# L2 pooling in windows of four: one instruction per load instead of two halves

## The chip, the cores and the metric

The kernel runs on one core of a Trainium2 chip. The metric is the device time of one execution in microseconds (us), the median of the runs shown. Four parts of the core matter here. ACT (ScalarE) and DVE (VectorE) are the engines that compute. SP (SyncE) computes nothing here and only issues transfers. The 16 DMA engines move data between HBM and SBUF.

## The reference

The input x has shape 32 x 256 x 4096 in float32, p is 2 and the window is 4. Each output element is the root of the mean of four squares:

```python
for i in range(out_length):                     # out_length = 4096 // 4
    window = np.abs(x[:, :, 4 * i:4 * i + 4]) ** 2.0
    result[:, :, i] = np.mean(window, axis=-1) ** 0.5
```

134.2 MB are read and 33.6 MB are written. Windows never cross a row, so the whole input can be treated as one flat run of windows.

## The kernel before, in words

The flat input is cut into 20 loads. Loads 0 to 18 bring 13184 elements (`W`) to each of 128 partitions, 6592 KB in all; load 19 brings the remaining 11648 per partition (`LAST`). Three slots in SBUF (`x_tiles`, shown as `xt`) take the loads in turn: load i goes to slot i mod 3. Load 0 is cut in two parts, the first of 1024 elements per partition on ACT's DMA queue. All other loads are issued on SP's queue.

The order on each engine is written out by hand, and each engine works through its own list in that order. For loads 0 to 17 the loop does the following, in two halves of 6592 elements per partition each:

- `square` (line 101, ACT) squares a half in place.
- `pairs` (line 107, DVE) adds elements 0 and 2, and 1 and 3, of each window, and writes the result in place to the front of the half.
- `fours` (line 111, DVE) adds the two sums of each window and writes 1648 elements to PSUM, to one of two tiles (`s_tiles`, shown as `st`), one for each half.
- `root` (line 114, ACT) scales by 1/4, takes the root and writes to the output tile `o_tile` (shown as `ot`). `roots(i)` runs both halves' roots.

`roots(i - 1)` stands on ACT between the two squares of load i. For i = 5, 9, 13 and 17 (`waits`) it stands behind both squares, and the pair sums of both halves come ahead of the sums of four, since at these places the root may have to wait.

`fours` of load i may overwrite the PSUM sums only when the roots of load i - 1 have read them. When `fours` of load i is done, its slot is free, and SP issues load i + 3 (line 87).

The output tile holds the results of four loads. The blocks of loads that are stored together are [0-3], [4-7], [8-11], [12, 13], [16, 17, 14, 15], [18] and [19]. Stores 0 to 3 are issued on ACT's queue (line 98), directly behind `roots` of loads 3, 7, 11 and 13. The first root of the next block writes where the store still reads, so it waits for the store to land.

The tail differs. Load 18 is squared in two parts, the first 5560 elements by a multiplication on DVE (line 151), the others on ACT. Load 19 goes through in three pieces of 6912, 3152 and 1584 elements. Stores 4, 5 and 6 (6592, 1648 and 1456 KB) are issued on SP's queue, behind `roots(17)`, behind the root of load 18, and behind the last root. The results of loads 18 and 19 lie in the slot of load 17.

Of the kernel before, what the change touches and what calls it, by code (L numbers as in the profile page):

```python
# [1 line left out]

# [4 lines left out]


@with_exitstack
def kernel(  # L10
    ctx: ExitStack,
    tc: tile.TileContext,
    x: bass.AP,
    p: float,
    kernel_size: int,
    out: bass.AP,
):

    nc = tc.nc

    assert float(p) == 2.0, "kernel specialized for p == 2"
    k = int(kernel_size)  # L30
    assert k == 4, "kernel specialized for kernel_size == 4"

    P = nc.NUM_PARTITIONS
    fp32 = mybir.dt.float32
    Act = mybir.ActivationFunctionType
    add = mybir.AluOpType.add
    xf = x.rearrange("b c l -> (b c l)")
    of = out.rearrange("b c l -> (b c l)")
    total = xf.shape[0] // P

    W = 13184
    H, R = W // 2, W // k
    X_SLOTS = 3
    EARLY = 1024
    LAST = total - 19 * W
    widths = [W] * 19 + [LAST]
    n = len(widths)
    assert 0 < LAST <= W and LAST % 16 == 0


    blocks = [[0, 1, 2, 3], [4, 5, 6, 7], [8, 9, 10, 11], [12, 13], [16, 17, 14, 15], [18], [19]]
    block_of = {i: b for b, loads in enumerate(blocks) for i in loads}
    block_width = [sum(widths[i] for i in loads) for loads in blocks]

    x_pool = ctx.enter_context(tc.tile_pool(name="x_pool", bufs=1))
    o_pool = ctx.enter_context(tc.tile_pool(name="o_pool", bufs=1))
    s_pool = ctx.enter_context(tc.tile_pool(name="s_pool", bufs=1, space=bass.MemoryType.PSUM))
    x_tiles = [x_pool.tile([P, W], fp32, name=f"xt{j}") for j in range(X_SLOTS)]
    o_tile = o_pool.tile([P, 4 * R], fp32, name="ot")
    first = o_pool.tile([P, 1], fp32, name="first")  # L60
    s_tiles = [s_pool.tile([P, 2048], fp32, name=f"st{j}") for j in range(2)]
    ctx.enter_context(tc.manual_schedule())

    def rows(flat, b, div):
        at = sum(block_width[:b]) * P // div
        return flat[at:at + block_width[b] * P // div].rearrange("(p w) -> p w", p=P)


    place = {}
    for b, loads in enumerate(blocks):  # L70
        for q, i in enumerate(loads):
            if i < 18:
                place[i] = o_tile[:, q * R:(q + 1) * R]
    free = x_tiles[17 % X_SLOTS]
    place[18] = free[:, 0:R]
    place[19] = free[:, R:R + LAST // k]

    xs = {}

    def load(i):  # L80
        b = block_of[i]
        at = sum(widths[j] for j in blocks[b][:blocks[b].index(i)])
        xs[i] = x_tiles[i % X_SLOTS][:, 0:widths[i]]
        cuts = [0, widths[i]] if i else [0, EARLY, W]
        queues = [nc.sync] if i else [nc.scalar, nc.sync]
        for queue, c, e in zip(queues, cuts, cuts[1:]):
            queue.dma_start(out=xs[i][:, c:e], in_=rows(xf, b, 1)[:, at + c:at + e])  # L87

    def store(b, queue):
        if b <= 2:  # L90
            held = o_tile[:, :]
        elif b == 3:
            held = o_tile[:, 0:2 * R]
        elif b == 4:
            held = o_tile[:, :]
        else:
            held = place[blocks[b][0]]
        queue.dma_start(out=rows(of, b, k), in_=held)

    def square(v):  # L100
        nc.scalar.activation(out=v, in_=v, func=Act.Square)  # L101

    def pairs(v):

        q = v.rearrange("p (n j) -> p n j", j=k)
        h = v[:, 0:v.shape[1] // 2].rearrange("p (n j) -> p n j", j=2)
        nc.vector.tensor_tensor(out=h, in0=q[:, :, 0:2], in1=q[:, :, 2:4], op=add)  # L107

    def fours(o, v):
        h = v[:, 0:v.shape[1] // 2].rearrange("p (n j) -> p n j", j=2)  # L110
        nc.vector.tensor_tensor(out=o, in0=h[:, :, 0], in1=h[:, :, 1], op=add)  # L111

    def root(o, s):
        nc.scalar.activation(out=o, in_=s, func=Act.Sqrt, scale=1.0 / k)  # L114

    def roots(i):
        for c in range(2):
            root(place[i][:, c * R // 2:(c + 1) * R // 2], s_tiles[c][:, 0:R // 2])
        if i in (3, 7, 11, 13):
            store(block_of[i], nc.scalar)  # L120

    for i in range(X_SLOTS):
        load(i)

    nc.vector.memset(first[:, :], 1.0)  # L125
    root(first[:, :], first[:, :])
    for i in range(18):
        halves = [xs[i][:, c * H:(c + 1) * H] for c in range(2)]
        waits = i > 1 and (i - 1) % 4 == 0
        square(halves[0])  # L130
        if i and not waits:
            roots(i - 1)
        square(halves[1])
        if waits:
            roots(i - 1)
            for v in halves:
                pairs(v)
            for c, v in enumerate(halves):
                fours(s_tiles[c][:, 0:R // 2], v)
        else:  # L140
            for c, v in enumerate(halves):
                pairs(v)
                fours(s_tiles[c][:, 0:R // 2], v)
        if i + X_SLOTS < n:
            load(i + X_SLOTS)
    roots(17)


    c = 5560
    v = xs[18][:, 0:c]  # L150
    nc.vector.tensor_tensor(out=v, in0=v, in1=v, op=mybir.AluOpType.mult)  # L151
    square(xs[18][:, c:W])
    store(4, nc.sync)
    for a, b in ((0, c), (c, W)):
        pairs(xs[18][:, a:b])
        fours(place[18][:, a // k:b // k], xs[18][:, a:b])
    ends = [0, 6912, 10064, LAST]
    for a, b in zip(ends, ends[1:]):
        v = xs[19][:, a:b]
        o = place[19][:, a // k:b // k]  # L160
        square(v)
        if a == 0:
            root(place[18], place[18])
            store(5, nc.sync)
        pairs(v)
        fours(o, v)
        if a:
            root(*last)
        last = (o, o)
    root(*last)  # L170
    store(6, nc.sync)


# [1 line left out]
_INS = ['x', 'p', 'kernel_size']  # L175
_OUTS = [((32, 256, 1024), 'float32')]

_NUMBERS = {'p': 2.0, 'kernel_size': 4}


# [26 lines left out]
```

## Time and profile before

| | |
|---|---|
| Time, median of 3 runs | 394.63 us (394.58 to 394.68) |
| Span of the profiled execution, first to last instruction | 392.7 us; its time outside the span is not in the profile |
| ACT busy | 279.3 us, 82 instructions |
| DVE busy | 223.4 us, 84 instructions |
| HBM read, written | 134.22 MB, 33.55 MB; 427 GB/s over the span |
| SP's DMA queue, ACT's DMA queue | 143.62 MB, 24.15 MB |

A profile line of a group of instructions gives the line of the kernel, the engine, the operation, what is written and read with their shapes (partitions x elements), the number of instructions, the busy time in us and the mean time of one in ns, and then the idle time of the engine just before them and what ended it. A line of DMA issues gives the tensors, the queue, the number, the size and the median time from issue to landing. In the timeline and in the chain of waits, the first two numbers are the start and the length in us, both from the start of the span.

### The profile page before, as it was taken

To read this page: it belongs to the slowest core of one execution; us is meant where nothing else is said; L and a number is where in the kernel's file an instruction comes from. 1 tells how busy PE (TensorE), PEld (TensorE's weight loads), DVE (VectorE), ACT (ScalarE), POOL (GpSimd) and SP (SyncE) were. 2 spreads that over 40 slices of the span, in tenths; PEclk is the share of its full clock that TensorE was granted. 3 is DMA by queue.
4 is the path that set the end of the run, shared out by engine and by line. 5 is a ranking of instruction groups with operands and counts; after the bars stand their busy time and mean duration, and the time that the engine had idled before them with its cause. 6 is when DMAs were issued, how large, how long until landed. Compare 5 with 4: busy or idle time off the path is not lost.

```text
span 392.7 us, 311 instructions
## 1 busy us (share of the span) xinstructions
DVE 223.4 (57%) x84; ACT 279.3 (71%) x82; POOL 0.2 (0%) x4
## 2 busy tenths in 40 slices
DVE  0046586766460567664606667645166654669992
ACT  1095988987650999876419898773297929897792
POOL 0000000000000000000000000000000000000000
DMA  8999999999999999999999999999999999999997
GB/s 337 436 430 430 430 440 440 435 457 376 430 430 430 446 430 440 430 440 440 446 430 436 435 435 431 435 430 430 430 430 419 457 414 430 435 429 451 415 428 320
DMA packets 4034, 167.79 MB, mean 427 GB/s; under 512 B 448, under 2 KB 448, under 8 KB 576
## 3 DMA queue, kind: packets, MB, share of 16 engines
q1 hardware_dynamic: 3312, 143.62, 84.9%
q10 hardware_dynamic: 720, 24.15, 14.2%
q14 instruction: 2, 0.02, 0.0%
HBM read 134.22 MB, written 33.55 MB: 427 GB/s over the span
## 4 chain that ended last, share of the span: by engine, by line
DMA 73%; ACT 17%; DVE 6%; issue 2%; SPq 0%; ACTq 0%; DVEq 0%
DMA xt<-in_x_dram 46%; DMA out_dram<-ot 27%; ACT xt L101 12%; ACT ot L114 5%; DVE xt L107 3%; DVE st L111 2%; DVE xt L111 1%; ACT xt L114 1%; SPq L87 0%; ACTq L101 0%; DVEq L107 0%; ACTq L114 0%
## 5 line engine op out<-in xcount | busy, mean ns | idle before, releaser
L101 ACT ACTIVATE xt<-xt 128x6592 f32<-128x6592 f32 (+4 forms) x40 | 221.4, 5547 | 61.2 <-DMA xt<-in_x_dram 59.6
L107 DVE TENSOR_TENSOR xt<-xt 128x3296 f32<-128x3296 f32 (+5 forms) x41 | 143.1, 3489 | 125.0 <-ACT xt L101 124.7
L111 DVE TENSOR_TENSOR st<-xt 128x1648 f32<-128x1648 f32 x36 | 67.4, 1882 | 36.0 <-ACT ot L114 34.1
L114 ACT ACTIVATE ot<-st 128x1648 f32<-128x1648 f32 x36 | 53.5, 1536 | 43.1 <-DMA out_dram<-ot 40.3
L111 DVE TENSOR_TENSOR xt<-xt 128x1390 f32<-128x1390 f32 (+4 forms) x5 | 7.3, 1452 | 0.2
L114 ACT ACTIVATE xt<-xt 128x3296 f32<-128x3296 f32 (+3 forms) x4 | 6.0, 1492 | 1.1 <-DVE xt L111 1.1
L151 DVE TENSOR_TENSOR xt<-xt 128x5560 f32<-128x5560 f32 x1 | 5.9, 5942 | 0.0
L114 ACT ACT_TABLE_LOAD x1 | 1.3, 1283 | 1.2 <-PEq L188 1.2
L125 DVE MEMSET first<- 128x1 f32 x1 | 0.1, 59 | 0.8 <-PEq L188 0.8
L114 ACT ACTIVATE first<-first 128x1 f32<-128x1 f32 x1 | 0.2, 202 | 0.0
L188 POOL MEMSET const-bfloat16-1.0<- 128x1 bf16 x1 | 0.1, 102 | 0.0
L188 POOL MEMSET const-uint8-127<- 128x1 uint8 x1 | 0.1, 102 | 0.0
L188 POOL MEMSET const-float32-0.0<- 128x1 f32 x1 | 0.1, 99 | 0.2 <-issue 0.2
L188 POOL MEMSET const-float32-1.0<- 128x1 f32 x1 | 0.1, 99 | 0.0
## 6 DMA issues: line engine op xcount, KB each, us to landing
xt<-in_x_dram SPq DMA_DIRECT2D x18, 6592.0 KB, 34.0
out_dram<-ot ACTq DMA_DIRECT2D x3, 6592.0 KB, 35.4
out_dram<-ot SPq DMA_DIRECT2D x1, 6592.0 KB, 24.8
xt<-in_x_dram SPq DMA_DIRECT2D x1, 6080.0 KB, 18.7
xt<-in_x_dram SPq DMA_DIRECT2D x1, 5824.0 KB, 25.2
out_dram<-ot ACTq DMA_DIRECT2D x1, 3296.0 KB, 27.7
out_dram<-xt SPq DMA_DIRECT2D x1, 1648.0 KB, 10.5
out_dram<-xt SPq DMA_DIRECT2D x1, 1456.0 KB, 5.8
```

The costliest lines, as they stand in the source:

```text
L101: nc.scalar.activation(out=v, in_=v, func=Act.Square)
L107: nc.vector.tensor_tensor(out=h, in0=q[:, :, 0:2], in1=q[:, :, 2:4], op=add)
L111: nc.vector.tensor_tensor(out=o, in0=h[:, :, 0], in1=h[:, :, 1], op=add)
L114: nc.scalar.activation(out=o, in_=s, func=Act.Sqrt, scale=1.0 / k)
L125: nc.vector.memset(first[:, :], 1.0)
L151: nc.vector.tensor_tensor(out=v, in0=v, in1=v, op=mybir.AluOpType.mult)
L188: nc = _bacc.Bacc("TRN2", target_bir_lowering=False, num_devices=1)
```

## The change

In the loop over loads 0 to 17, each load is now handled whole. There is one square of 13184 elements, one sum of pairs that writes 6592, one sum of fours that writes 3296 and one root of 3296, where there were two of each. The two PSUM tiles become one of 4096 elements, of which 3296 are used. `roots(i - 1)` always stands directly behind the square of load i, and the case `waits` is gone. Loads, slots, blocks, the places of the stores in the program and the tail are the same.

```diff
     W = 13184
-    H, R = W // 2, W // k
+    R = W // k
...
-    s_tiles = [s_pool.tile([P, 2048], fp32, name=f"st{j}") for j in range(2)]
+    s_tile = s_pool.tile([P, 4096], fp32, name="st")
...
     def roots(i):
-        for c in range(2):
-            root(place[i][:, c * R // 2:(c + 1) * R // 2], s_tiles[c][:, 0:R // 2])
+        root(place[i], s_tile[:, 0:R])
         if i in (3, 7, 11, 13):
             store(block_of[i], nc.scalar)
...
     for i in range(18):
-        halves = [xs[i][:, c * H:(c + 1) * H] for c in range(2)]
-        waits = i > 1 and (i - 1) % 4 == 0
-        square(halves[0])
-        if i and not waits:
+        square(xs[i])
+        if i:
             roots(i - 1)
-        square(halves[1])
-        if waits:
-            roots(i - 1)
-            for v in halves:
-                pairs(v)
-            for c, v in enumerate(halves):
-                fours(s_tiles[c][:, 0:R // 2], v)
-        else:
-            for c, v in enumerate(halves):
-                pairs(v)
-                fours(s_tiles[c][:, 0:R // 2], v)
+        pairs(xs[i])
+        fours(s_tile[:, 0:R], xs[i])
         if i + X_SLOTS < n:
             load(i + X_SLOTS)
     roots(17)
```

## The prediction

> **What bounds the kernel now.** I read the page first: engine shares, slices, chain, DMA issues.
>
> ```profile
> DVE 223.4 (57%) x84; ACT 279.3 (71%) x82; POOL 0.2 (0%) x4
> DMA  8999999999999999999999999999999999999997
> DMA 73%; ACT 17%; DVE 6%; issue 2%; SPq 0%; ACTq 0%; DVEq 0%
> ...
> out_dram<-ot SPq DMA_DIRECT2D x1, 6592.0 KB, 24.8
> ...
> out_dram<-xt SPq DMA_DIRECT2D x1, 1648.0 KB, 10.5
> out_dram<-xt SPq DMA_DIRECT2D x1, 1456.0 KB, 5.8
> ```
>
> The 16 DMA engines are at 90% or more in all but the first and last slice, while ACT and DVE idle 29% and 43%. The timeline shows two unshared loads taken up at 66.25 and 81.83 us: 15.58 us for 6,750,208 bytes, 433 GB/s. The three last stores, issued on SP at 359.48, 377.75 and 385.87, land (add the last column) at 384.3, 388.2 and 391.7. The last two take 3.9 us for 1.69 MB and 3.5 us for 1.49 MB, which is 430 GB/s again: the last store was issued 2.3 us before the one ahead of it had landed. So transfers run without a hole up to the end, and a cheaper instruction gains nothing. The question is whether a later one opens a hole.
>
> Prices come from the groups by form:
>
> ```profile
> L101 ACT ACTIVATE xt<-xt 128x6592 f32<-128x6592 f32 x36 | 204.6, 5696 | 58.3 <-DMA xt<-in_x_dram 56.6 <-ACT ot L114 1.7
> L107 DVE TENSOR_TENSOR xt<-xt 128x3296 f32<-128x3296 f32 x36 | 129.3, 3593 | 124.4 <-ACT xt L101 124.3
> L111 DVE TENSOR_TENSOR st<-xt 128x1648 f32<-128x1648 f32 x36 | 67.4, 1882 | 36.0 <-ACT ot L114 34.1
> L114 ACT ACTIVATE ot<-st 128x1648 f32<-128x1648 f32 x36 | 53.5, 1536 | 43.1 <-DMA out_dram<-ot 40.3 <-DVE st L111 2.8
> ...
> L107 DVE TENSOR_TENSOR xt<-xt 128x1576 f32<-128x1576 f32 x1 | 1.8, 1793 | 0.0
> ...
> L101 ACT ACTIVATE xt<-xt 128x1584 f32<-128x1584 f32 x1 | 1.5, 1506 | 0.0
> ...
> L111 DVE TENSOR_TENSOR xt<-xt 128x788 f32<-128x788 f32 x1 | 1.0, 980 | 0.0
> ```
>
> Two sizes of each give slope and fixed part. DVE's largest idle time waits for squares (124.3 us), ACT's for loads and, 40.3 us, for stores. The chain of waits prices a store that shares the engines with loads, and the timeline (start, us) gives the tail:
>
> ```profile
> 90.42 36.48 DMA out_dram<-ot
> 168.83 35.44 DMA out_dram<-ot
> 246.87 35.01 DMA out_dram<-ot
> ```
>
> ```profile
> 339.39 11.28 ACT L101 ACTIVATE xt<-xt 128x6592 f32<-128x6592 f32 x2 [1.43 <-DMA xt<-in_x_dram]
> 357.79 5.94 DVE L151 TENSOR_TENSOR xt<-xt 128x5560 f32<-128x5560 f32 x1
> 377.75 8.46 SPq L98 DMA_DIRECT2D out_dram<-xt  x2
> 385.32 0.53 ACT L114 ACTIVATE xt<-xt 128x396 f32<-128x396 f32 x1 [0.91 <-DVE xt L111]
> ```
>
> **The wide instructions.** 72 instructions go: 18 each of square, pair sum, four sum and root. No trace row has the square, pair sum and four sum at full width, so I extend the rows. Square: slope (5696-1506)/(6592-1584) = 0.837 ns, so 5.70 + 6592 x 0.837 ns = 11.2 us. Pairs: slope (3593-1793)/(3296-1576) = 1.047 ns, 7.04 us. Fours: slope (1882-980)/(1648-788) = 1.049 ns, 3.61 us. Root: 1.54 + 1648 x 0.837 ns = 2.9 us; the only root of 3296 in the trace, from SBUF, took 2.95. Back to back, ACT starts the next one 0.1 us before the last one's end (two squares in 11.28), so it needs 11.1 + 2.9 = 14.0 us a load, as before, and DVE 10.65 instead of 10.95. The bounds are twice the half's time from above and the slope alone (square 11.0, pairs 6.9, fours 3.45) from below. I take the fitted values. No row suggests that a root reading a PSUM tile of 3296 costs more per element: at 1648 it follows the square's slope to within 0.03 us.
>
> The page "Advanced Engine Details and Errata", section The Read-Write Bubble, says that each ACT and DVE instruction exposes the memory's latency once and advises large tiles; the fits agree, with fixed parts of 0.18 us (square) and 0.14 us (pairs). Taken alone it would make the kernel faster by an estimated 36 x 0.1 + 36 x 0.15 = 9 us, to about 386, but the trace has both engines idle and transfers bounding, so none of it is taken.
>
> **What is lost: the halves' overlap.** DVE could start after half a square; now it starts after a whole one. A load's slot was released 19.7 us after the square's start (66.25 to 86.00, where SP issues the next load). Now: 11.2 + 7.04 + 3.61 + 0.1 = 21.95, 2.2 us later. Between stores that is hidden: when a slot comes free, one load has landed and another runs until 31.2 us after the first one's landing, 9 us of cover. Without that cover it would cost up to 2.2 us a load.
>
> **Stores.** The store of a block stood behind the roots that ran between two half squares, 8.6 us after its load (81.83 to 90.42). Now it stands behind a whole square and a root, 14.0 us: issue at 95.9, 5.5 us later. The store takes 35.0 to 36.5 us (rows above; the first one's 36.5 and the mean of 35.6 give 36 for the first). It then holds up root(4), and behind it on ACT every later square, on DVE fours(5), and on SP the load into that slot. Call its landing S. Then load(8) is issued at S + 2.9 + 3.6 + 0.1 = S + 6.6 (before S + 5.35), load(9) at S + 2.9 + 11.1 + 10.65 + 0.1 = S + 24.7 (before 22.7), and the next store at S + 2.9 + 3 x 14.0 = S + 44.9. Before it was S + 41.9, with ACT waiting 1.5 us for a load on the way. So a block now takes ACT and its store 44.9 + 35.4 = 80.3 us, against 5 x 15.58 = 77.9 of transfers: each block loses 2.4 us of the cover. S runs 132, 212.3, 292.6 (before 126.9, 204.3, 281.9); with stores of 35.0 or 36.5 throughout, 130.9/210.8/290.7 or 132.4/213.8/295.2.
>
> Two places have little cover left. Load(13) is issued at 212.3 + 24.7 = 237.0 (235.5 to 238.5); load(12) lands at 238.2 as before (a load step of the chain: 209.63 + 28.56), the same bytes having gone by. Load(16) is issued at 292.6 + 6.6 = 299.2 (297.3 to 301.8); load(15) ends at 238.2 + 4 x 15.58 = 300.5. A load needs a lead: with the first issue at 0.73, the windows show no transfer in 0 to 1 us and full rate in 1 to 2, so 0.3 to 1.3 us; I take 1.0. And the transfer ends before the landing is signalled: the last window with traffic is 390 to 391, the landing 391.7, so 0.5 us. The deadlines are then about 236.7 and 299.0. Holes together: none with short stores, 2.5 with long ones; in the middle the sums miss by 0.3 and 0.2, and I take 0.6.
>
> **The tail.** Load(17) lands at 339.4 + hole, ACT being free at about 338. fours(17) ends 21.9 later, at 361.3, where it ended at 357.9: 3.4 late. Behind it on DVE stands all the work on loads 18 and 19, without a gap from 357.79 to the pairs at 374.82, so the last root moves along: before, 385.85 - 357.88 = 28.0 us after fours(17), now 389.25. What that delays: load(19), issued 345.7 instead of 343.56, is covered by load(18), which lands at 355 (339.4 + 15.6); store(4), 364.2 instead of 359.48, by load(19) ahead of it on SP's queue, landing at 368.7; store(5), 381.2, by store(4), running until 384.3. Store(6) is not covered: issued at 389.25, when store(5) has landed at 388.2. Its end: 389.25 + 1.0 lead + 3.5 transfer + 0.5 to the signal = 394.25, against 391.7: 2.5 late.
>
> The page "DMA: Bandwidth & Descriptors", section Latency and other measured facts, gives about 0.6 us from issue to first byte for queues of this kind; by that the end would come 0.4 us earlier. No window here resolves it.
>
> **Sum.** Span 392.7 + 2.5 (tail) + 0.6 (holes) = 395.8. Outside the span the median has 394.63 - 392.7 = 1.9 us: 397.7.
>
> **Rivals.** *Covered (no change).* The last store comes in time if it is issued by about 386.7 (388.2 less lead and signal); its delay must stay under 0.8 of the 3.4 us. That needs load(17)'s 21.9 us shortened by 2.6, wide instructions 12% cheaper per element than the rows. For it: no row has them. Against it: three sizes of each lie on one line. It gives 394.6. *Faster.* The holes that the kernel has are at its start and end, about 1 us each; a tail that ran earlier could save at most that, 393.5, and needs the same cheap instructions, 20% off. *The ACT cycle decides.* With stores of 36.5 us (the first one's row), the lag grows by 3.5 a block and the two holes sum to 2.5: 394.63 + 2.5 + 2.5 = 399.6, and 400.5 with a lead of 1.3 instead of 1.0 at all three places. It decides from stores over about 36 us each; two of the three rows lie under that. *A wide instruction is run as two:* then the chain is 0.3 us longer, 398.0, inside the forecast.
>
> **Chances.** Forecast 0.72; ACT cycle 0.18; covered 0.07; faster 0.03. The range goes from 396.4 (no hole, lead 0.3) to 400.5 (the long stores and leads). A difference of 0.2%, 0.8 us, is about what can be told from none: faster 0.03, same 0.07, slower 0.90.
>
> **What would show it.** Squares of 13184 at 11.2 us, pairs of 6592 at 7.0, x18 each; first store issued near 95.9, ACT's waits for stores ending near 132, 212 and 293; the DMA row full until the last slices; the last store landing about 5 us after its issue at 389 to 390, on a chain that ends in DVE and ACT. A full DMA row to the end, or the last store issued before 387, would prove the tail's step wrong; loads landing later than 238.2 (12) and 339.4 (17) by over 2 us would mean the holes are larger.

## The result, and the profile after

The changed kernel takes 401.29 us (median of 4 runs, 401.08 to 402.59) against 394.65 us; the ratio is 1.0172, 95% interval 1.0159 to 1.0184. It is 6.6 us slower. The forecast was 397.7 us with a range to 400.5: the sign was right, the size was not, and the time lies outside the range. In all comparisons, executions more than 1.5% above the fastest of the same kernel are left out; this matters for one experiment below (e6), whose executions spread from 394.96 to 401.3 us.

The page of the changed kernel, with the lines that answer to those of before:

```profile
DVE 218.0 (55%) x48; ACT 275.2 (69%) x46; POOL 0.2 (0%) x4
DMA  8999999999999999999999999999999999999994
DMA 48%; ACT 37%; DVE 13%; issue 0%; SPq 0%; ACTq 0%; DVEq 0%
...
out_dram<-ot SPq DMA_DIRECT2D x1, 6592.0 KB, 20.0
...
out_dram<-xt SPq DMA_DIRECT2D x1, 1648.0 KB, 7.0
out_dram<-xt SPq DMA_DIRECT2D x1, 1456.0 KB, 4.9
```

Both engines are busy for less time (ACT 4.1, DVE 5.4 us) and the kernel is still slower. ACT's share of the chain has gone from 17% to 37%. The DMA row looks as full as before until the last slice. The last store lands 4.9 us after its issue, not 5.8: it now finds an empty queue.

The groups by form show the wide instructions at the forecast prices (11.2, 7.04, 3.61 and 2.9 us):

```profile
L101 ACT ACTIVATE xt<-xt 128x13184 f32<-128x13184 f32 x18 | 201.4, 11189 | 34.6 <-DMA xt<-in_x_dram 34.2 <-ACT ot L114 0.4
L107 DVE TENSOR_TENSOR xt<-xt 128x6592 f32<-128x6592 f32 x18 | 126.4, 7025 | 112.6 <-ACT xt L101 112.6
L111 DVE TENSOR_TENSOR st<-xt 128x3296 f32<-128x3296 f32 x18 | 64.8, 3600 | 61.0 <-ACT ot L114 59.5
L114 ACT ACTIVATE ot<-st 128x3296 f32<-128x3296 f32 x18 | 52.4, 2910 | 79.9 <-DMA out_dram<-ot 71.9 <-DVE st L111 8.0
```

ACT's wait for stores has grown from 40.3 to 71.9 us, and DVE's wait for ACT's roots behind them from 34.1 to 59.5. The chain of waits (start, us) has the three long stores and the load of slot 17, and the timeline has the tail:

```profile
95.58 36.47 DMA out_dram<-ot
...
176.74 35.23 DMA out_dram<-ot
...
256.66 36.30 DMA out_dram<-ot
...
317.82 25.89 DMA xt<-in_x_dram
```

```profile
343.74 11.19 ACT L101 ACTIVATE xt<-xt 128x13184 f32<-128x13184 f32 x1 [5.60 <-DMA xt<-in_x_dram]
...
365.60 5.95 DVE L139 TENSOR_TENSOR xt<-xt 128x5560 f32<-128x5560 f32 x1
...
385.56 8.23 SPq L98 DMA_DIRECT2D out_dram<-xt  x2
...
392.90 0.53 ACT L114 ACTIVATE xt<-xt 128x396 f32<-128x396 f32 x1 [0.90 <-DVE xt L111]
```

Load 17 lands at 343.72 (317.82 + 25.89), 4.35 us later than before. From there to the landing of the last store (issued at 393.46, landed at 398.33) it takes 54.6 us, where before it took 391.71 - 339.37 = 52.3. So 4.35 us come from the middle of the kernel and 2.3 from its tail.

Where the middle loses them, the same windows of both kernels show (us: DVE, ACT and POOL busy, clock, DMA share, GB/s). First before, then after:

```profile
145.00:175.00 30.00, 20.99 (x9) 28.00 (x8) 0.00 (x0) 1.00 1.02 443
175.00:225.00 50.00, 25.35 (x9) 30.67 (x9) 0.00 (x0) 1.00 0.99 428
225.00:255.00 30.00, 20.33 (x8) 26.04 (x8) 0.00 (x0) 1.00 1.02 442
255.00:305.00 50.00, 25.16 (x10) 31.04 (x9) 0.00 (x0) 1.00 0.99 429
```

```profile
145.00:175.00 30.00, 22.32 (x5) 30.00 (x6) 0.00 (x0) 1.00 1.00 424
175.00:225.00 50.00, 20.18 (x4) 25.84 (x4) 0.00 (x0) 1.00 1.00 424
225.00:255.00 30.00, 22.40 (x5) 30.00 (x6) 0.00 (x0) 1.00 1.00 422
255.00:305.00 50.00, 20.10 (x4) 24.78 (x4) 0.00 (x0) 1.00 0.99 422
```

The DMA share is 0.99 or more in every one of these windows, yet less goes through: 30 x 19 + 50 x 4 + 30 x 20 + 50 x 7 = 1720 GB/s x us, which is 1.7 MB or 4.0 us of transfer. A window counts a whole row (one partition's 52,736 bytes) where the row starts, and a round of 16 rows is 0.84 MB, or 28 GB/s in 30 us. So a single window proves little, the sum over all four is good to about a round (1.95 us), and the records of single rows, used below, say it better. Busy DMA engines moved less. That is the point where the prediction had no term. In the windows from 145 to 175 and from 225 to 255 ACT is busy without a pause (30.00 of 30 us).

### The profile page after: what moved, and what is told of

Same layout as the page of the kernel before. It is cut to its first block, busy times and chain, and to the rows that moved or that the text cites. A ratio compares the mean times of both kernels' runs of the same rounds, so it can differ in the third digit from the quotient of the medians.

```text
span 399.3 us, 210 instructions
## 1 busy us (share of the span) xinstructions
DVE 218.0 (55%) x48; ACT 275.2 (69%) x46; POOL 0.2 (0%) x4
## 4 chain that ended last, share of the span: by engine, by line
DMA 48%; ACT 37%; DVE 13%; issue 0%; SPq 0%; ACTq 0%; DVEq 0%
ACT xt L101 29%; DMA out_dram<-ot 27%; DMA xt<-in_x_dram 21%; DVE xt L107 7%; ACT ot L114 7%; DVE st L111 3%; DVE xt L139 1%; ACT xt L114 1%; DVE xt L111 1%; SPq L87 0%; ACTq L114 0%; DVEq L111 0%
## 5 line engine op out<-in xcount | busy, mean ns | idle before, releaser
L101 ACT ACTIVATE xt<-xt 128x13184 f32<-128x13184 f32 (+4 forms) x22 | 218.1, 9919 | 34.6 <-DMA xt<-in_x_dram 34.2
L107 DVE TENSOR_TENSOR xt<-xt 128x6592 f32<-128x6592 f32 (+5 forms) x23 | 140.2, 6094 | 112.9 <-ACT xt L101 112.7
L114 ACT ACTIVATE ot<-st 128x3296 f32<-128x3296 f32 x18 | 52.4, 2910 | 79.9 <-DMA out_dram<-ot 71.9
L111 DVE TENSOR_TENSOR st<-xt 128x3296 f32<-128x3296 f32 x18 | 64.8, 3600 | 61.0 <-ACT ot L114 59.5
## 6 DMA issues: line engine op xcount, KB each, us to landing
out_dram<-ot ACTq DMA_DIRECT2D x3, 6592.0 KB, 36.3
```

## The experiments

Two theories stood at the start. *Lateness*: the middle is lost because stores, and the loads behind them, are issued late. *Wide traffic*: the wide instructions themselves slow the transfers beside them. Ratios are to the kernel before on the same chip.

**The tail alone, and the middle alone (e1, e2).** Each load can be handled in halves, as before, or whole; e1 handles only load 17 whole, e2 all but load 17. The diffs of e1 to e6 and of e12 are given in short form; e1 to e6 all keep the one PSUM tile of the change.

```diff
-        square(xs[i]) ... pairs(xs[i]) ... fours(s_tile[:, 0:R], xs[i])      # for every i
+        # e1: whole for i == 17 only, halves in the order of before otherwise
+        # e2: whole for i < 17, halves for i == 17
```

> Only load 17 is handled whole; loads 0 to 16 stay in halves, in the order of before. Both theories: load 17 lands at 339.4 as before, its sums end 3.4 us later, and the last store is issued after the one ahead of it has landed: 2.3 to 2.6 us over before, 397.1. Were the tail covered after all: 394.6.

Measured: 396.89 us, ratio 1.0054 (1.0039 to 1.0069). Its timeline:

```profile
339.71 11.19 ACT L106 ACTIVATE xt<-xt 128x13184 f32<-128x13184 f32 x1 [1.50 <-DMA xt<-in_x_dram]
...
361.57 5.95 DVE L165 TENSOR_TENSOR xt<-xt 128x5560 f32<-128x5560 f32 x1
```

Load 17 comes when it came before (339.7 instead of 339.4), and the DVE work on load 18 begins at 361.57 instead of 357.79. One load of eighteen handled whole costs 2.3 us: the tail's term is shown.

> Loads 0 to 16 whole as in the changed kernel, load 17 in halves. Both theories: load 17 still lands at about 343.7, the last store comes 3.4 us earlier and is covered again, so 2.2 us under the changed kernel: 399.1. The part over before that then stays (4.4 us) is the middle's alone.

Measured: 399.91 us (398.15 to 400.87), ratio 1.0139 (1.0114 to 1.0163). The tail's part is gone, and 5.3 us remain, with a spread of 2.7 us between executions of one kernel. With e1's 2.3 us this makes 7.6, not 6.6; the spread is wide enough for the difference.

**Earlier stores (e3, e4).**

```diff
-        square(xs[i])
-        if i:
-            roots(i - 1)
+        if i in (4, 8, 12, 14):
+            square(halves[0]); roots(i - 1); square(halves[1])   # the store stands behind these roots
+        else:
+            square(xs[i]); roots(i - 1)
```

> As the changed kernel (whole pair sums, sums of four and roots), but the squares of loads 4, 8, 12 and 14 are in halves with the root between them, so each store is issued 5.5 us earlier and ACT's way from store to store is back at 41.9 us or less. Lateness theory (the middle is lost because stores and, behind them, loads 9, 13 and 16 are issued late): load 17 lands at 339.4 to 339.9 and only the tail's loss stays, 396.9 to 397.5. Wide-traffic theory (the wide instructions themselves slow the transfers that run beside them): no change in the middle, 400.5 to 401.3.

Measured: 396.69 us, ratio 1.0049 (1.0034 to 1.0064). Its windows, to be held against those above:

```profile
145.00:175.00 30.00, 17.07 (x4) 27.29 (x5) 0.00 (x0) 1.00 1.03 445
175.00:225.00 50.00, 27.80 (x5) 31.15 (x6) 0.00 (x0) 1.00 0.99 430
225.00:255.00 30.00, 16.29 (x5) 25.68 (x5) 0.00 (x0) 1.00 1.02 441
255.00:305.00 50.00, 24.39 (x5) 30.96 (x6) 0.00 (x0) 1.00 0.99 429
```

With all sums whole, the transfers are back at the rates of before (in sum, 0.1 MB more than before).

> Early stores as in the run before it, and load 17 in halves. Lateness theory: both losses are gone although 17 of 18 loads have whole sums, 394.5 to 395.0. Wide-traffic theory: 398.4 to 399.2.

Measured: 394.78 us, ratio 1.0004 (0.9995 to 1.0013). Seventeen of eighteen loads have whole sums, thirteen have whole squares, and no difference can be told. Wide traffic has fallen: what costs is the time at which things are issued, in two places, the tail (2.3) and the stores with the loads behind them (the rest). e3 and e4 moved both: load 13 was issued at 229.2 in e3, not 236.84 as in the changed kernel.

**What of the lateness costs (e5 to e11).** The next runs were to tell whether the price is paid where a load is issued too late for the queue, as the prediction had it, or at the stores. Where the text speaks of rows or of the 16 completions, it goes by the trace's records of single DMA packets, which no view prints. e5 restores the early store at load 4 alone:

```diff
-        if i in (4, 8, 12, 14):
+        if i == 4:
```

> As the changed kernel, but the square of load 4 alone is in halves with the root between them: the first store is issued at about 91 instead of 95.6, the others stand as in the changed kernel. Cover theory (lateness costs only once it exceeds the cover of one transfer; the lag of 2.4 us a block then uses up only what the first store gives back): loads 9, 13 and 16 are issued 4 us or more before the transfers ahead of them end, load 17 lands at 339.4 to 340, and the tail's loss alone stays: 396.6 to 397.3. Per-store theory (each store that comes late costs its share, about a third of 4.4 us): 399.5 to 400.

Measured: 398.08 us (397.96 to 399.79), ratio 1.0100 (1.0079 to 1.0120). Load 17 lands at 340.1. So one earlier store takes back 3.6 of the middle's 4.35 us: nearer to the cover theory, but 0.8 us above its range. e5 also issues load 13 at 233.96, 2.9 us earlier, and its records show no hole there.

e6 has no wide instruction, only the changed order on ACT:

```diff
         square(halves[0])
-        if i and not waits:
-            roots(i - 1)
         square(halves[1])
-        if waits:
-            roots(i - 1)
+        roots(i - 1)
...
+            # both pairs, then both fours, for every i
```

> Everything in halves (no wide instruction), but the roots of the load before always stand behind both half squares, as in the changed kernel; both pair sums come ahead of both sums of four. First store at 95.9, ACT's way from store to store 44.9 us as in the changed kernel; load 13 is issued near 234, load 17's chain is that of before. Load theory (the price is paid where a load is issued too late for the queue): middle and tail both covered, 394.5 to 395.2. Store theory (the price is paid at the late stores themselves): 397.5 to 399.

Measured: ten executions between 394.96 and 401.3 us, median 399.85; ratio 1.0096 (1.0066 to 1.0126). Both theories are hit by one execution or another. In the profiled one (401.3, one of the two left out) loads 12, 13 and 16 were issued within about 2 us of the queue's end, so it does not decide. The ten times show that the order alone, without a wide instruction, can cost nearly as much as the whole change (400.51 us, with 394.71 before) or next to nothing (394.96).

e7, e8 and e10 keep the order of before and delay one load, e9 another:

```diff
+        if i == 10:                       # e9: i == 1
+            v = xs[i][:, 0:N]             # N = 9500 (e7), 11400 (e8), 7600 (e10), 10000 (e9)
+            nc.vector.tensor_tensor(out=v, in0=v, in1=v, op=mybir.AluOpType.mult)
         if i + X_SLOTS < n:
             load(i + X_SLOTS)
```

> The kernel before with one more DVE instruction (9500 elements of the freed slot, multiplied in place) ahead of load 13's issue alone, so that it comes at 237.0 as in the changed kernel, not at 227; all else in the order of before. The step of the prediction (deadline 236.7): 0.3 us of hole and no more, 394.9. Restart theory (a load that finds the queue nearly dry also runs its first rows slower): 1.0 to 1.6 us, 395.6 to 396.2.

Measured: 398.07 us, ratio 1.0086 (1.0069 to 1.0103); load 13 was issued at 237.6.

> The same with 11400 elements, load 13 issued at 239.0. The step of the prediction: 2.3 us, 396.9. Restart theory: 3.0 to 3.6 us, 397.6 to 398.2.

Measured: 399.19 us, ratio 1.0120 (1.0105 to 1.0136); issued at 238.55.

> The kernel before with load 13 issued at about 235.3 (7600 elements), 2 us ahead of the end of load 12's rows. Hole theory, with a lead of 1.0 us: covered, 394.5 to 395.0. If a queue with one short remainder also costs (rows slower though never dry): 395.5 to 397.

Measured: 396.75 us, ratio 1.0043 (1.0030 to 1.0056); issued at 234.8, with over 2 us of cover.

> The kernel before with one more DVE instruction (10000 elements of the freed slot, multiplied in place) ahead of load 4's issue, so that it comes at about 65.3, as late against load 3's end as load 13 was at 237.6; but here the next store comes 25 us later, not 12. Hole alone: 1.2 us, 395.8. Hole and slow first rows: 1.8 us, 396.4. The full price of the run with load 13 at 237 (3.4 us, a constant of any dry queue): 398.0.

Measured: 397.19 us, ratio 1.0060 (1.0047 to 1.0073); issued at 65.1.

None fits "hole and no more". In the packet records of e7, the first rows of load 13 start 1.0 us after its issue (the assumed lead), run 0.6 us longer than the usual 1.95, and the rows in flight when store 2 comes run 1.3 us longer again; in e9 the first rows of load 4 run 0.7 us longer. The DMA engines were without a row for 1.6, 2.7 and 1.3 us each in e7, e8 and e9, and the runs lost 3.4, 4.5 and 2.4 us: a late load cost 1.7 to 2.2 times its hole. But the extra instruction also delays the store that follows (store 2 at 250.06 in e7, not 246.87; even e10 moves it, by 0.4), so these runs do not separate load from store.

e11 does: only the first store is moved (the next two follow, 3.7 and 5.0 us later than before, through ACT's waits), every load keeps over 2 us of cover up to the second store, and there is no wide instruction.

```diff
         square(halves[0])
-        if i and not waits:
+        if i and not waits and i != 4:
             roots(i - 1)
         square(halves[1])
+        if i == 4:
+            roots(i - 1)
```

> The kernel before, but the roots of load 3 stand behind both half squares of load 4, so that the first store alone is issued 5.5 us later, at 95.9. Load and cover theory: every load is still issued 4 us or more before the queue runs out, 394.4 to 395.0; the rows that ran long when the first store came at 90.4 (0.8 us a DMA engine) may fall away, 393.9. Store theory (a store pays for coming late): 395.8 to 396.5.

Measured: 402.04 us (399.73 to 405.66), ratio 1.0192 (1.0154 to 1.0231): slower than the whole change. Its chain and one window:

```profile
95.90 36.96 DMA out_dram<-ot
...
172.48 39.80 DMA out_dram<-ot
...
251.90 39.67 DMA out_dram<-ot
```

```profile
175.00:225.00 50.00, 20.47 (x9) 27.38 (x9) 0.00 (x0) 1.00 0.99 391
```

The second store, now at 172.48 instead of 168.83, takes 39.8 us instead of 35.4, and while it shares the DMA engines they move 391 GB/s at a share of 0.99. The loss is made there and not at the store that was moved: the mean of the 16 completions of load 8, behind the first store, is 159.15 (before 159.62), that of load 12, behind the second, 241.50 (before 237.56). The load theory, and with it the prediction's idea of where the price is paid, has fallen as the whole story.

**Transfers alone (e12, e13).**

```diff
-    square / roots / pairs / fours
+    nc.scalar.activation(out=first, in_=xs[i][:, 0:1], func=Act.Square)   # waits for the landing
+    if i in delays: timer(us); store(block, nc.scalar)                    # set to 1, 5, 9, 13 us
     load(i + X_SLOTS)
```

> Transfers alone: the loads and stores of the kernel, no squares, sums or roots (the output is a constant). A load is issued as soon as the load three before it has landed, so the queue always holds two or more; a timer on ACT issues four full stores 1, 5, 9 and 13 us after loads 3, 7, 11 and 15 have landed. Phase theory (a store that comes near the boundary of two loads slows the rows): the stores at 1 and 13 us cost 1 us or more each, those at 5 and 9 under 0.3; 396 to 398. Depth theory (stores cost only where few loads are queued): none costs over 0.3 after the first, 394.4 to 395.4.

> The same with the delays 13, 1, 5 and 9 us in this order, so that place in the program and phase can be told apart. Phase theory: the first and second store cost, 396 to 398. Depth theory: 394.4 to 395.4.

Measured, one execution each: 400.74 and 398.9 us, with 394.54 for the kernel before. By the trace, the four delays were 0.1, 4.0, 9.7 and 13.4 us, as the store is issued while the timer's last instruction still runs (in e12 at 66.12, the timer from 66.17 to 67.02); the text goes on to call them 1, 5, 9 and 13. The page of e12:

```profile
DMA  8999999999999999999999999999999999999992
```

The queue is never short, no load is squared or summed, the same bytes go through, and it takes 6.2 and 4.4 us longer. The completions say how. Each transfer is spread over 16 DMA engines and has landed when the last of them has finished. For the last store the mean of the 16 is 391.65 and 391.75, about as before (391.14), but the last one comes at 397.90 and 396.05. A straggling engine, not the mean, sets the time. The distance from the first to the last of a load's 16 completions, well behind each store, tells which store did it: in e12 it is 0.9 us at the start and 1.2, 1.4, 1.4 and 7.1 behind the stores at 1, 5, 9 and 13 us; in e13 it is 0.8, then 3.0 behind 13 us, 4.6 behind 1, 5.5 behind 5 and 5.9 behind 9. The depth theory has fallen. The phase theory is half right: 13 us after a landing, 2.1 before the next, is the worst place in both, but the same delay costs 5.7 and 2.2 us, and 1 us costs 0.2 and 1.6. By the mean, though, these runs with a full queue lost only 0.5 and 0.6 us, so they do not show where the changed kernel's loss by the mean comes from, which is told below.

**Without sharing (e14 to e16).**

```diff
         if i in (3, 7, 11, 13):
-            store(block_of[i], nc.scalar)
+            store(block_of[i], nc.sync)
```

> The changed kernel with stores 0 to 3 issued on SP's queue instead of ACT's, at the same point behind their roots. A store then goes through behind the loads that are queued, and no DMA engine changes between a load's rows and a store's. The first store is still issued at 95.6. Sharing theory (the middle is lost where two queues share the DMA engines and rows stretch): no row is stretched, load 17 lands at 339 to 340, only the tail's loss stays, 396.5 to 397.3. Lateness theory (the stores' time of issue itself): 400 to 402.

Measured: 398.71 us (397.57 to 399.44), ratio 1.0102 (1.0082 to 1.0122). The first store is issued at 95.64, as in the changed kernel, but load 17 lands at 340.62, not 343.72. Windows:

```profile
145.00:175.00 30.00, 23.00 (x5) 28.89 (x5) 0.00 (x0) 1.00 1.02 443
175.00:225.00 50.00, 21.54 (x5) 29.02 (x5) 0.00 (x0) 1.00 0.99 426
225.00:255.00 30.00, 22.99 (x5) 28.02 (x5) 0.00 (x0) 1.00 1.03 445
255.00:305.00 50.00, 21.20 (x5) 29.53 (x5) 0.00 (x0) 1.00 0.99 425
```

> The same with load 17 in halves, so that the tail is covered as before. Sharing theory: 393.8 to 394.8, as the kernel before or up to 0.8 us faster, since the rows that it loses at its first store (0.8 us a DMA engine) fall away too. Lateness theory: 398 to 400.

Measured: 396.21 us, ratio 1.0042 (1.0030 to 1.0055).

> The kernel before, stores 0 to 3 on SP's queue, nothing else. Sharing theory: 393.7 to 394.2, for the 0.8 us at its first store. Lateness theory: 394.6.

Measured: 396.79 us, ratio 1.0050 (1.0038 to 1.0063): slower than the kernel before, against both expectations.

With the stores on one queue with the loads, whole (e14) and halves (e16) differ by 1.9 us, the tail, and with the tail covered (e15) whole is no slower than halves. The stores' time of issue costs nothing there, 5.2 us late or not. The middle's loss falls from the changed kernel's 4.35 us to 1.25 (load 17 at 340.62), of which e16 has 1.1 with nothing late (340.49); by the mean of the 16 completions (339.14 in e14, 339.01 in e16, 338.77 before) next to nothing is lost. But this does not show that the loss needs the sharing. In e14 the stores also take only 33 us, so loads 9 and 13 come at 154.0 and 232.0 instead of 156.9 and 236.8, and the late loads are gone with the sharing. Nor do long rows need two queues: in e14 to e16 too, the row in flight on each DMA engine as the first store's turn came ran 0.7 to 0.8 us longer (at 109 us), so the expected gain of 0.8 us did not come. No version measured beats the kernel before; e4 equals it.

## Why the prediction was wrong in size

*Prices of the wide instructions*: right to 0.02 us.

*ACT's schedule around the stores*: right. First store 95.58 (forecast 95.9), stores landed at 132.05, 211.97 and 292.96 (132, 212.3, 292.6), load 13 issued at 236.84 (237.0), load 16 at 299.62 (299.2).

*The tail*: right. The forecast had 394.25 - 339.4 = 54.85 us from load 17's landing to the end, measured 54.6; e1 shows the term alone, 2.3 for 2.5. Its lead of 1.0 us was 0.84 (the last store was issued at 393.46, its first row starts at 394.30).

*The holes*: this is the step that failed. The prediction had 0.6 us, at most 2.5; load 17 came 4.35 us late. The holes as the prediction defined them are there at about their size, though not quite at its places: the packet records show the 16 DMA engines without a row for 0.2 and 0.35 us each on average, ahead of load 9 and load 13 and not of load 13 and load 16.

What failed is the sentence that load 12 "lands at 238.2 as before, the same bytes having gone by". It landed at 240.28. The sum took the transfers for a stream of 433 GB/s that can only be filled or left empty. In the changed kernel the rows of that stream ran longer (by 0.8 us in all 16 engines as store 1 came, by 0.9 as store 2 came), and stragglers held back each landing: the 16 completions of load 17 have a mean of 341.92 and a last one at 343.72, where before they had 338.77 and 339.37. So 3.1 us of the 4.35 are lost by the mean and 1.2 by the stragglers. Held against before, the records of rows and holes add up to the 3.1: holes 0.5, longer rows behind the two late loads 1.1, longer rows at stores 1 and 2 1.9, other rows 0.4, less 0.75 that before loses at its first store and the changed kernel does not. The bounds did not hold it because they moved the stores' length and the lead, but never the rate.

Two smaller points. The deadlines go by the landing of the last DMA engine, while most engines run dry earlier (load 12's completions before have a mean of 237.56, 0.6 ahead of the last). And the hole with long stores is 301.8 - 299.0 = 2.8 by the prediction's own figures, not 2.5, which would put the upper end at 400.8, still below the result. Its sign for larger holes, loads 12 and 17 over 2 us late, came up (2.1 and 4.3), but what it stands for did not: the holes were 0.5.

*The rivals*: "the ACT cycle decides" came nearest in time (399.6), by a lag of stores over 36 us; they took 36.5, 35.2 and 36.3, and the lag was the forecast's own. Its time was near for another reason. "Covered" and "faster" were refuted by e1.

What is shown: the tail's 2.3 us (e1, e3, e4); that the rest comes from the times of the stores and of the loads behind them and goes when they are put back (e3, e4); that a change of order alone can lose as much, without a late load (e11); that transfers with a full queue and next to no computation can lose 4 to 6 us by stragglers (e12, e13).

What stays open: why rows run longer and why an engine falls behind. A short queue is not needed for stragglers (e12, e13). For the loss by the mean, the larger part of the changed kernel's, it may be. In the profiled runs of after, e2, e7, e8 and e10, where load 13 was issued between 234.8 and 238.6, the rows in flight as store 2 came ran 0.95 to 1.35 us longer per DMA engine; in before, e1, e3, e4, e5 and e9, where it was issued by 234.0, at most 0.05; e6 lies between (235.4, 0.3). Against it stands e11, where 113 rows of loads and store took over 2.1 us, 2.5 on average, all through the second store, with no load late.

A place shortly before the load in progress lands was bad for the second store of e11, in e12 and e13, and for the second and third store of the changed kernel (0.6 us ahead of a landing). But the first stores of e11 and of the changed kernel (1.3 and 1.5 us ahead) cost nothing by the mean, and the second and third of e5 came there too, with load 17 only 0.8 us late. No run of the changed kernel separates its late loads from its late stores. Whether the rows' addresses or the engines' positions against each other decide it was not tried.

The page "DMA: Bandwidth & Descriptors" of the Trainium skill, section Queues, rings and completion order, says that a DMA engine takes turns between the queues it has work for, and its section Why a DMA increments its semaphore by 16 and not by 1 says that only the full 16 means that all data has landed. The runs agree with both: in the shared stretches of e12 rows of load and store alternate on an engine (1.95 us each), and the slowest engine's completion is the landing (343.72 for load 17, mean 341.92). The section Issuing engines are not separate DMA queues says that issuing on several engines only saves the sequencer's time; here the same stores moved from ACT to SP changed the time by -2.6 us (e14 against the changed kernel) and by +2.1 us (e16 against before), so in these runs it is not all.

## What to carry to other kernels

Before fusing two half instructions into one, look for what is issued behind them: the engines got 4 and 5 us cheaper here and it was worth nothing, while the last store's issue (3.2 us later behind load 17) and the first one's (5 us later) were on the path. The tail can be costed by walking the chain behind the last load (right to 0.3 us here). Where loads and stores share the DMA engines in a kernel that runs at the transfers' rate, that rate is not given once a store moves: measure it, in several executions, since they spread by 3 to 6 us in e2, e6 and e11.

## What the runs showed of the hardware

A row of 52,736 bytes takes one DMA engine 1.95 us in nearly all packet records, and the few longer ones made up 2.65 of the 3.15 us by which load 17's mean completion was late. At the arrival of a store, the row in flight on each engine could run 0.7 to 1.4 us longer (also in the kernel before, 0.85 at its first store), or not at all; behind a late load the first rows ran 0.6 to 0.7 us longer (e7, e8, e9). A single DMA engine could fall 5 to 6 us behind the other fifteen with all of them busy (e12: mean completion 391.65, the last two 392.37 and 397.90), and nothing later gave it back: the distance from the first to the last completion stayed at 7.1 us over the last four transfers. A DMA share of 0.99 stood beside 391 GB/s in one window (e11) and beside 430 in the same window of another kernel (e3): the share says that the engines were busy, not that they moved data at full rate.
